# Down projections of an encoder trunk: activations held still and weights moved, with seven products over all inner chunks

## The chip, the cores and the metric

The kernel runs on one core of a Trainium2 chip. The core has a matrix engine (TensorE, PE in the profile), a vector engine (VectorE, DVE), an activation engine (ScalarE, ACT), a general engine (GpSimd, POOL) and a queue engine for transfers (SyncE, SP). Matmuls write into PSUM banks; everything else works in SBUF. The metric is the device time of one execution in microseconds, the median of several runs.

## The reference

The program is a two-layer bidirectional encoder on 512 tokens of width 1024 in float32. Each layer adds, in turn, half of a SwiGLU feed-forward block, an attention mixer, half of a second feed-forward block, and a gated embedding of the layer's own input. Four feed-forward blocks are run in all:

```python
def swiglu(x, w_gate, w_up, w_down):
    return (jax.nn.silu(x @ w_gate) * (x @ w_up)) @ w_down

h = h + 0.5 * swiglu(rmsnorm(h, norm_ffn1[i]), ffn1_w_gate[i], ffn1_w_up[i], ffn1_w_down[i])
```

The inner width is 2816, which is 22 chunks of 128. The down projection is the last product, 512 x 2816 by 2816 x 1024.

## The kernel before

The hidden state is kept feature by token: chunk c of `h` is a tile of 128 features by 512 tokens. Every float32 operand of a matmul is split into a high and a low part (`split`, lines 149 to 151: ScalarE copies the rounded high part, VectorE subtracts it), and every product is made of three matmuls: high by high, high by low and low by high. All weights are split on the chip as they arrive. A raw weight tile (`wr`, five buffers) holds 128 x 1024 numbers, its parts `wh` and `wl` have four buffers each. Activation tiles of 128 x 512 come from a pool `act` of 62 buffers, scratch tiles from `tmp` with eight.

`ffn` first makes the 22 inner chunks, `pair_fast` (line 331) for most of them: gate and up products by a scheme of seven half-size products in place of eight, with sums of weights made partly by an accumulating DMA on GpSimd's queue (line 341). Each chunk is split into `a[m] = (high, low)`, and the first eight are also written to DRAM.

`down` (line 421) then makes the eight output chunks of 128 features by 512 tokens. Weights are the stationary operand and activations move. Output chunks 0 and 1 are plain: 22 inner chunks, three matmuls of 512 columns each (`plain`, lines 440 to 442). Output chunks 2 to 7 go in pairs: the first eight inner chunks by seven products of 256 columns (`product`, lines 484 to 486, with sums of weights from `inner_weights` and of activations from `inner_sums`), the other fourteen plainly. As an output chunk ends, `evict` (line 448) adds half of it to `h`, stores it, and gives the norm's input split (`norm_split`, lines 201 and 202) and its square sum (`norm_square`, line 216, mostly on GpSimd) to the next stage. The next stage (attention projections after the first block of a layer, the gated embedding after the second) starts with `project` or `mm_unit` on these split chunks (`mm3`, lines 175 to 177).

Nothing here writes out the queues by hand, except for a few marked places. A planner orders the instructions of each engine ahead of time, in the program's order of priority and by its own estimate of when inputs and buffers are ready. On the chip each engine then runs its queue strictly in that order, and an instruction whose semaphore is not there yet holds what is behind it.

## Time and profile before

| | |
|---|---|
| median of three runs | 2040.51 us (2040.38 to 2041.76) |
| span of the profiled execution, first to last instruction | 2039.8 us |
| TensorE busy | 2018.5 us, 99% |
| VectorE busy | 1510.8 us, 74% |
| ScalarE busy | 1056.6 us, 52% |
| GpSimd busy | 269.2 us, 13% |
| mean DMA rate | 153 GB/s |

The profile names a group of instructions by its line in the kernel, its engine, its operation and its tiles (output, arrow, inputs). The profiled execution carries no second clock: its own time is the span in the table, 0.7 us under the median of the runs. Matmuls are pipelined, so their durations overlap each other, and the step from one start to the next tells their price.

### The profile page before, as it was taken

How to read it: one execution, taken by the hardware profiler on the slowest of the kernel's cores; microseconds unless marked ns; L12 is line 12 of the kernel's file. 1: busy time of each engine (PE TensorE's matmuls, PEld its weight loads, DVE VectorE, ACT ScalarE, POOL GpSimd, SP SyncE). 2: the span in 40 equal slices, each digit the busy share in tenths (PEclk: the TensorE clock that was granted, in tenths of full speed). 3: DMA queues.
4: the chain of work that ended last, by engine and by line, in shares of the span. 5: the costliest groups of instructions: out<-in, count | busy, mean ns of one | idle time of the engine just before them, and what ended most of it. 6: DMA issues, size and time to landing. Idle time of an engine off the chain costs nothing.

```text
span 2039.8 us, 33724 instructions
## 1 busy us (share of the span) xinstructions
PE 2018.5 (99%) x12862; PEld 1820.6 (89%) x12862; DVE 1510.8 (74%) x2575; ACT 1056.6 (52%) x1798; POOL 269.2 (13%) x306
## 2 busy tenths in 40 slices
PE   9999999999999999999999999999999999999998
PEld 6999988878888899988888999888888889998886
DVE  8888865598766888875568888755778688888554
ACT  6555543377644555553445555434666545555342
POOL 1100011342212110001211100021000111000111
PEclk9999999999999999999999999999999999999999
DMA  7776644543424477653545765545333446665451
GB/s 222 192 187 184 186 142 159 143 98 73 100 72 165 134 197 183 170 191 123 184 152 154 197 182 158 191 143 154 110 104 110 155 127 188 184 180 164 132 204 42
DMA packets 122354, 312.93 MB, mean 153 GB/s; under 512 B 23504, under 2 KB 31184, under 8 KB 122192
## 3 DMA queue, kind: packets, MB, share of 16 engines
q1 hardware_dynamic: 102336, 249.91, 37.6%
q0 software_dynamic: 19712, 60.83, 15.4%
q8 instruction: 101, 1.65, 0.3%
q14 instruction: 61, 0.50, 0.1%
q10 hardware_dynamic: 144, 0.04, 0.0%
HBM read 274.02 MB, written 25.66 MB: 147 GB/s over the span
## 4 chain that ended last, share of the span: by engine, by line
PE 90%; DVE 3%; DMA 2%; ACT 2%; issue 1%; POOL 1%; SPq 0%; DVEq 0%; POOLq 0%; ACTq 0%
PE mm L365 6%; PE mm L364 6%; PE mm L363 6%; PE mm L176 6%; PE mm L177 6%; PE mm L175 6%; PE mm L440 5%; PE mm L441 5%; PE mm L442 5%; PE sc L364 3%; PE sc L363 3%; PE sc L365 3%; PE sc L175 3%; PE sc L177 3%; PE sc L176 3%; PE ob L365 2%
## 5 line engine op out<-in xcount | busy, mean ns | idle before, releaser
L150 ACT ACTIVATE wh<-wr 128x1024 fp32r<-128x1024 f32 (+2 forms) x455 | 465.6, 1026 | 533.6 <-PE mm L441 162.6
L151 DVE TENSOR_TENSOR wl<-wr,wh 128x1024 fp32r<-128x1024 f32 (+2 forms) x455 | 538.3, 1187 | 193.5 <-ACT wh L150 189.9
L365 PE MATMUL mm<-act,wl 128*128 128x256 f32 x1088 | 307.9, 283 | 0.0
L364 PE MATMUL mm<-act,wh 128*128 128x256 f32 x1088 | 307.9, 283 | 0.0
L363 PE MATMUL mm<-act,wh 128*128 128x256 f32 x1088 | 307.9, 283 | 0.0
L175 PE MATMUL mm<-act,wh 128*128 128x512 f32 (+1 forms) x648 | 254.0, 393 | 1.0 <-ACT wh L150 0.5
L176 PE MATMUL mm<-act,wh 128*128 128x512 f32 (+1 forms) x648 | 254.1, 392 | 0.6 <-DVE act L202 0.6
L177 PE MATMUL mm<-act,wl 128*128 128x512 f32 (+1 forms) x648 | 253.7, 392 | 0.0
L364 PEld LDWEIGHTS mm<-act,wh 128*128 128x128 f32 x1088 | 208.8, 192 | 0.3
L363 PEld LDWEIGHTS mm<-act,wh 128*128 128x128 f32 x1088 | 208.9, 192 | 0.2
L365 PEld LDWEIGHTS mm<-act,wl 128*128 128x128 f32 x1088 | 208.9, 192 | 0.2
L440 PE MATMUL mm<-act,wh 128*128 128x512 f32 x512 | 199.4, 389 | 0.0
L441 PE MATMUL mm<-act,wh 128*128 128x512 f32 x512 | 199.4, 389 | 0.0
L442 PE MATMUL mm<-act,wl 128*128 128x512 f32 x512 | 199.2, 389 | 0.0
L150 ACT ACTIVATE act<-tmp 128x512 fp32r<-128x512 f32 (+1 forms) x204 | 113.9, 590 | 85.5 <-DVE tmp L524 36.8
L363 PE MATMUL sc<-act,wh 128*128 128x256 f32 x544 | 154.0, 283 | 0.0
L364 PE MATMUL sc<-act,wh 128*128 128x256 f32 x544 | 154.0, 283 | 0.0
L365 PE MATMUL sc<-act,wl 128*128 128x256 f32 x544 | 154.0, 283 | 0.0
L176 PEld LDWEIGHTS mm<-act,wh 128*128 128x128 f32 x648 | 122.2, 189 | 24.7 <-DVE act L202 2.0
L175 PEld LDWEIGHTS mm<-act,wh 128*128 128x128 f32 x648 | 122.2, 189 | 23.8 <-ACT wh L150 1.0
L177 PEld LDWEIGHTS mm<-act,wl 128*128 128x128 f32 x648 | 122.2, 189 | 22.0 <-DVE wl L151 0.2
L151 DVE TENSOR_TENSOR act<-tmp,act 128x512 fp32r<-128x512 f32 (+1 forms) x200 | 125.4, 641 | 10.4 <-ACT act L150 8.8
(225 smaller groups left out, 4431.7 us busy)
## 6 DMA issues: line engine op xcount, KB each, us to landing
wr<-in_gu_dram SPq DMA_DIRECT2D x176, 512.0 KB, 4.6
wr<-in_gu_dram POOLq DMA_DIRECT2D x68, 512.0 KB, 5.5
wr<-in_dn_dram SPq DMA_DIRECT2D x64, 512.0 KB, 3.9
rb<-in_gu_dram SPq DMA_DIRECT2D x68, 256.0 KB, 2.9
wr<-in_dn_dram SPq DMA_DIRECT2D x32, 384.0 KB, 3.3
wr<-in_qk_ab_dram SPq DMA_DIRECT2D x20, 512.0 KB, 3.5
inner<-tmp POOLq DMA_DIRECT2D x32, 256.0 KB, 3.1
tmp<-inner SPq DMA_DIRECT2D x32, 256.0 KB, 4.4
```

Of the source, the lines that this page charges most:

```text
L150: self.put(self.nc.scalar.activation(hi, src, AF.Copy))
L151: self.put((lo_eng or self.nc.vector).tensor_tensor(lo, src, hi.bitcast(F32), op=ALU.subtract))
L175: mm(out, stat[0], mov[0], start=start, stop=False)
L176: mm(out, stat[0], mov[1], start=False, stop=False)
L177: return mm(out, stat[1], mov[0], start=False, stop=stop)
L363: mm(out, w[0][:, c], xs[k][0][:, x], start=start and k == 0, stop=False, skip_group_check=True)
L364: mm(out, w[0][:, c], xs[k][1][:, x], start=False, stop=False, skip_group_check=True)
L365: mm(out, w[1][:, c], xs[k][0][:, x], start=False, stop=stop and k == half - 1, skip_group_check=True)
L440: mm(p, u[0][:, c], xh, start=start and j == 0, stop=False, skip_group_check=True)
L441: mm(p, u[0][:, c], xl, start=False, stop=False, skip_group_check=True)
L442: mm(p, u[1][:, c], xh, start=False, stop=s + j == NF - 1, skip_group_check=True)
```

## The change

The down projection is turned around. A tile of activations (128 inner by 128 tokens) is now the stationary operand, and the weights move, 512 output columns at a time, so that an output block is 128 tokens by 512 features. Tokens, inner width and output width are each cut in two, and the whole product is made of seven products of quarter blocks (256 tokens, 11 inner chunks, 512 features) in four sections. The first section makes two products per weight quarter, the second one, the third three, the fourth one. Sums of weight quarters are made in the raw tile by accumulating DMAs on GpSimd's queue (`add`), sums of activations by GpSimd's own operations in place (`pool`), and VectorE and ScalarE split every result. `ffn` no longer splits the inner chunks, nor writes them to DRAM. The weights are laid out on the host as four quarters.

The output quarters are put together on ScalarE and VectorE, turned back to feature by token with 32 transposes on TensorE (`turned`), and added to `h` (`done`), for the last four chunks in token halves, so `norm_split` takes a range of tokens. `mm_units` is new: the stages that follow make their first two projections together, chunks 0 to 3 for both, then chunks 4 to 7.

```diff
...
 FRONT = 4
 FAST = range(5, NF)
 SUMS = 0, 1, 2, 3
-SEVEN = 4
-LATER = 3, 4, 5
-READY = 3
+K2 = NF // 2
 UP_AT = 3
 LEAD = 6
 ACTS = 62
...
         mm(out, stat[0], mov[1], start=False, stop=False)
         return mm(out, stat[1], mov[0], start=False, stop=stop)
-    def mm_unit(self, out, u, xs, start, stop):
-        for i, x in enumerate(xs):
+    def mm_unit(self, out, u, xs, start, stop, ks=None):
+        for i in ks or range(len(xs)):
             w = (u[0][:, i * P:(i + 1) * P], u[1][:, i * P:(i + 1) * P])
-            self.last_mm = self.mm3(out, w, x, start and i == 0, stop and i == len(xs) - 1)
+            self.last_mm = self.mm3(out, w, xs[i], start and i == 0, stop and i == len(xs) - 1)
+    def mm_units(self, outs, us, between=None):
+        half = KC // 2
+        for ks in (range(half), range(half, KC)):
+            for out, u in zip(outs, us):
+                self.mm_unit(out, u, self.xg, True, True, ks)
+            if between:
+                between()
+                between = None
     def begin_norm(self, k):
...
         self.norm_split(c)
         self.norm_square(c)
-    def norm_split(self, c):
-        nc = self.nc
-        h, g = self.h[c], self.gain[:, self.k, c:c + 1]
+    def norm_split(self, c, x=slice(0, T)):
+        nc = self.nc
+        h, g = self.h[c][:, x], self.gain[:, self.k, c:c + 1]
         if self.k < N_NORM - 1:
-            hi, lo = self.act(F32R), self.act(F32R)
-            ins = (self.put(nc.scalar.activation(hi, h, AF.Copy, scale=g)),
-                   self.put(nc.vector.scalar_tensor_tensor(lo, h, g, hi.bitcast(F32), op0=ALU.mult, op1=ALU.subtract)))
-            self.xg[c] = (hi, lo)
-            return ins
+            if self.xg[c] is None:
+                self.xg[c] = self.act(F32R), self.act(F32R)
+            hi, lo = (y[:, x] for y in self.xg[c])
+            return (self.put(nc.scalar.activation(hi, h, AF.Copy, scale=g)),
+                    self.put(nc.vector.scalar_tensor_tensor(lo, h, g, hi.bitcast(F32), op0=ALU.mult, op1=ALU.subtract)))
     def norm_square(self, c):
         nc = self.nc
...
         a, y, t = [], [None] * KC, [None] * (KC // 2)
         kept = io["xT"].rearrange("p c t -> c p t") if first else self.put_away()
-        raw = self.dp.tile([2 * SEVEN, P, T], F32, name=self.nm("inner"))
         for m in range(NF):
             if m < FRONT:
                 r = self.pair_front(gu[i, m], m, first, gu[i, m + 1])
...
                 r = self.pair_fast(gu[i, m], y, t)
             else:
                 r = self.pair(gu[i, m], y)
-            if m < 2 * SEVEN:
-                nc.gpsimd.dma_start(raw[m], r)
-            ah, al = self.act(F32R), self.act(F32R)
-            self.split(r, ah, al)
-            a.append((ah, al))
+            a.append(r)
             for c, after in enumerate(SUMS):
                 if m == after:
                     y[c], y[c + KC // 2], t[c] = self.halves(c)
         self.begin_norm(k_next)
-        self.down(dn[i], a, raw, kept)
-    def down(self, w, a, raw, kept):
+        self.down(dn[i], a, kept)
+    def down(self, w, a, kept):
         nc, H = self.nc, T // 2
         l, r = slice(0, H), slice(H, T)
         self.kept = self.dp.tile([KC, P, T], F32, name=self.nm("kept"))
...
+        copy, tt, sub = nc.scalar.activation, nc.vector.tensor_tensor, ALU.subtract
+        pool = nc.gpsimd.tensor_tensor
+        b11, b12, b21, b22 = (w[n] for n in range(4))
+        units = [slice(u, min(u + 2, K2)) for u in range(0, K2, 2)]
+        ks = lambda u: range(u.start, u.stop)
+        def load(b, u):
+            raw = self.wr.tile([P, UNIT], F32, tag="wr", name=self.nm("wr"))[:, :(u.stop - u.start) * T]
+            nc.sync.dma_start(raw, b[:, u.start * T:u.stop * T])
+            return raw
+        def add(raw, b, u):
+            nc.gpsimd.dma_start(raw, b[:, u.start * T:u.stop * T], accum_op=ALU.add)
+        def product(out, u, ws, xs, cols, start, stop):
+            mm = nc.tensor.matmul
+            for j, k in enumerate(ks(u)):
+                wh, wl = (x[:, j * T:(j + 1) * T] for x in ws)
+                for i, p in enumerate(out):
+                    c = slice(cols.start + i * P, cols.start + (i + 1) * P)
+                    xh, xl = (x[:, c] for x in xs[k])
+                    mm(p, xh, wh, start=start and k == 0, stop=False, skip_group_check=True)
+                    mm(p, xh, wl, start=False, stop=False, skip_group_check=True)
+                    mm(p, xl, wh, start=False, stop=stop and k == K2 - 1, skip_group_check=True)
+        def copied(p):
+            out = [self.act() for _ in p]
+            for o, x in zip(out, p):
+                copy(o, x, AF.Copy)
+            return out
+        r1, r3 = [self.bank(), self.bank()], [self.sbank(), self.sbank()]
+        x1, x2, x3, x4 = ([None] * K2 for _ in range(4))
+        for u in units:
+            raw = load(b11, u)
+            for k in ks(u):
+                pool(a[k][:, r], a[k][:, r], a[K2 + k][:, r], op=sub)
+                x1[k] = self.split_chunk(a[k], nc.vector)
+            product(r1, u, self.parts(raw), x1, l, True, True)
+            add(raw, b12, u)
+            product(r3, u, self.parts(raw), x1, r, True, True)
+        c1, c5 = copied(r1), copied(r3)
+        r2 = [self.bank(), self.obank()]
+        for u in units:
+            raw = load(b21, u)
+            for k in ks(u):
+                x2[k] = self.split_chunk(a[K2 + k], nc.vector)
+            product(r2, u, self.parts(raw), x2, l, True, True)
+        for o, p in zip(c1, r2):
+            tt(o, p, o, op=ALU.add)
+        c11 = c1
+        rb, rc = [self.tbank(), self.tbank()], [self.bank(), self.obank()]
+        for u in units:
+            raw = load(b12, u)
+            add(raw, b22, u)
+            for k in ks(u):
+                pool(a[k][:, r], a[k][:, r], a[k][:, l], op=sub)
+                pool(a[k][:, l], a[k][:, r], a[K2 + k][:, r], op=ALU.add)
+                x3[k] = self.split_chunk(a[k], nc.vector)
+                pool(a[K2 + k][:, l], a[K2 + k][:, l], a[k][:, r], op=ALU.add)
+            product(rb, u, self.parts(raw), x3, l, True, True)
+            add(raw, b11, u)
+            product(r1, u, self.parts(raw), x3, r, False, True)
+            add(raw, b21, u)
+            product(rc, u, self.parts(raw), x2, r, True, True)
+        c2, c21 = copied(r1), [self.act(), self.act()]
+        u3 = [self.act(), self.act()]
+        for i in range(2):
+            tt(u3[i], c2[i], rb[i], op=sub)
+            tt(c21[i], rc[i], u3[i], op=ALU.add)
+            tt(c5[i], c5[i], u3[i], op=sub)
+        c22 = c5
+        hs = []
+        for m in range(KC):
+            hs.append(self.act())
+            nc.sync.dma_start(hs[m], kept[m])
+        for u in units:
+            raw = load(b22, u)
+            for k in ks(u):
+                hi, lo = self.act(F32R), self.act(F32R)
+                self.split(a[K2 + k][:, l], hi[:, l], lo[:, l])
+                x4[k] = hi, lo
+            product(r3, u, self.parts(raw), x4, l, False, True)
+        def turned(out, x, j):
+            for i, y in enumerate(x):
+                nc.tensor.transpose(out[:, i * P:(i + 1) * P], y[:, j * P:(j + 1) * P], self.ident)
+        def done(m, p, c):
+            h = hs[m]
+            nc.vector.scalar_tensor_tensor(h[:, c], p, 0.5, h[:, c], op0=ALU.mult, op1=ALU.add)
             self.h[m] = h
-            if m not in LATER:
+            if c.stop == T and c.start == 0:
                 self.norm_split(m)
+            else:
+                self.norm_split(m, c)
+        M = KC // 2
+        for m in range(M):
+            p = self.tbank()
+            turned(p[:, l], c11, m)
+            turned(p[:, r], c21, m)
+            done(m, p, slice(0, T))
+            nc.gpsimd.dma_start(self.kept[m], hs[m])
             self.norm_square(m)
...
+        for m in range(0, M, 2):
+            p = self.tbank()
+            for j in range(2):
+                turned(p[:, j * H:(j + 1) * H], c22, m + j)
+            for j in range(2):
+                done(M + m + j, p[:, j * H:(j + 1) * H], r)
+        for c in (l, r):
+            for i in range(2):
+                tt(c2[i][:, c], r3[i][:, c], c2[i][:, c], op=sub)
+        for m in range(0, M, 2):
+            p = self.tbank()
+            for j in range(2):
+                turned(p[:, j * H:(j + 1) * H], c2, m + j)
+            for j in range(2):
+                done(M + m + j, p[:, j * H:(j + 1) * H], l)
+        for m in range(M, KC):
+            nc.gpsimd.dma_start(self.kept[m], hs[m])
+            self.norm_square(m)
     def parts(self, raw):
         n = raw.shape[-1]
...
-        p = [self.project(w[12 + i], self.sbank()) for i in range(2)]
+        p = [self.obank(), self.bank()]
+        self.mm_units(p, [self.unit(w[12 + i], lo_eng=self.lo_eng()) for i in range(2)])
...
+        first = [self.obank(), self.bank()]
+        self.mm_units(first, [self.unit(io["qk_c"][i], lo_eng=self.lo_eng()) for i in range(2)])
         fill, steps = [], []
         for n in range(KC):
-            fill += [(("q", n), 1, lambda n=n: proj_q(n)), (("k", n), 1, lambda n=n: proj_k(n))]
+            fill += [(("q", n), 1, lambda n=n: proj_q(n, None if n else first[0])),
+                     (("k", n), 1, lambda n=n: proj_k(n, None if n else first[1]))]
...
-        up, ends = None, []
+        up, ends, first = None, [], []
         for m in range(KC):
             self.fetch(self.kept, m)
-            u = self.unit(io["plg"][i, m])
+            u = first[m][0] if m < len(first) else self.unit(io["plg"][i, m])
             if m % 4 == 0:
                 up = self.unit(io["plp"][i, m // 4])
             s = m % 4 * 2 * P
             upm = tuple(x[:, s:s + 2 * P] for x in up)
+            if m == 0:
+                first = [(u, self.bank(), self.obank()), (self.unit(io["plg"][i, 1]), self.bank(), self.sbank())]
+                def inner():
+                    for j, (_, _, q) in enumerate(first):
+                        self.mm_unit(q, tuple(x[:, j * 2 * P:(j + 1) * 2 * P] for x in up), p, True, True)
+                self.mm_units([f[1] for f in first], [f[0] for f in first], inner)
             half = k_next == N_NORM - 1 and m == KC - 1
             for x in (slice(0, T // 2), slice(T // 2, T)) if half else (slice(0, T),):
                 cut = lambda parts: [tuple(y[:, x] for y in c) for c in parts]
-                pg, pp = self.bank()[:, x], self.sbank()[:, x]
-                self.mm_unit(pg, u, cut(xg), True, True)
-                self.mm_unit(pp, upm, cut(p), True, True)
+                if m < len(first):
+                    pg, pp = first[m][1:]
+                else:
+                    pg, pp = self.bank()[:, x], self.sbank()[:, x]
+                    self.mm_unit(pg, u, cut(xg), True, True)
+                    self.mm_unit(pp, upm, cut(p), True, True)
                 if m == 0:
                     R = self.R
                     self.begin_norm(k_next)
...
     return np.concatenate([u[:, :, D // 2:], u[:, :, :D // 2], g], axis=2)
+def _quarters(w):
+    return w.reshape(2, K2, P, 2, T).transpose(0, 3, 2, 1, 4).reshape(4, P, K2 * T)
 def _rows(w):
     k, m = w.shape
...
     for n, (wg, wu, wd) in (("1", (ffn1_w_gate, ffn1_w_up, ffn1_w_down)),
                             ("2", (ffn2_w_gate, ffn2_w_up, ffn2_w_down))):
         a["gu" + n] = np.stack([_pairs(wg[i], wu[i]) for i in range(DEPTH)])
-        a["dn" + n] = np.stack([_tiles(wd[i]) for i in range(DEPTH)])
+        a["dn" + n] = np.stack([_quarters(wd[i]) for i in range(DEPTH)])
```

More of the change, by code (lines that the diff above doesn't have):

```diff
@@ L282, in pair_front @@
         R = self.R
-        t1, t2 = self.tmp(), self.tmp()
+        t1, t2 = self.tmp(), self.act()
         nc.vector.tensor_tensor(t1, pgu[0], R, op=ALU.mult)
@@ L304, in pair @@
             pgu.append(p)
-        t = self.tmp()
+        t = self.act()
         nc.scalar.activation(t, pgu[0], AF.Silu)
```

109 lines of the change are left out of this document (5 added, 104 removed).

## Prediction

> **What bounds the kernel now.** I read the shares of the engines first, then the groups of the down projection, then the order of time around one of its four calls.
>
> ```profile
> span 2039.8 us, 33724 instructions
> PE 2018.5 (99%) x12862; PEld 1820.6 (89%) x12862; DVE 1510.8 (74%) x2575; ACT 1056.6 (52%) x1798; POOL 269.2 (13%) x306
> L440 PE MATMUL mm<-act,wh 128*128 128x512 f32 x512 | 199.4, 389 | 0.0
> L484 PE MATMUL mm<-act,wh 128*128 128x256 f32 x144 | 40.8, 283 | 0.0
> L484 PE MATMUL sc<-act,wh 128*128 128x256 f32 x144 | 40.7, 283 | 0.0
> L484 PE MATMUL ob<-act,wh 128*128 128x256 f32 x48 | 13.6, 283 | 0.0
> ```
>
> TensorE is never free, and the last column says that no matmul of the down projection waited. Three lines (440 to 442) issue 512 matmuls each of 512 columns, three (484 to 486) issue 336 each of 256 columns: 384 and 252 in each call. Their mean durations (389 and 283 ns) overlap, so a matmul's price is the step from one start to the next:
>
> ```profile
> 237.97 0.28 PE L364 MATMUL mm<-act,wh 128*128 128x256 f32 x1
> 238.09 0.28 PE L365 MATMUL mm<-act,wl 128*128 128x256 f32 x1
> 238.22 0.40 PE L440 MATMUL mm<-act,wh 128*128 128x512 f32 x1
> 238.45 0.40 PE L441 MATMUL mm<-act,wh 128*128 128x512 f32 x1
> ...
> 354.45 0.39 PE L441 MATMUL mm<-act,wh 128*128 128x512 f32 x1
> 355.36 0.39 PE L442 MATMUL mm<-act,wl 128*128 128x512 f32 x1
> 355.58 0.39 PE L175 MATMUL sc<-act,wh 128*128 128x512 f32 x1
> ```
>
> 256 columns step by 0.12 us, 512 by 0.2275 (354.45 to 355.36 is four steps). The call runs from 238.22 to 355.58, 117.4 us; 384 x 0.2275 + 252 x 0.12 = 117.6. So the call is matmul steps and nothing else, and a split of weights or activations, a DMA or a sum costs nothing as long as it stays beneath them. The change is worth what it takes from the steps, less what it brings out from beneath.
>
> **The change, part by part.**
>
> *Matmuls.* All 22 chunks go through seven products of 11 chunks, two blocks of 128 tokens and three terms: 7 x 11 x 2 x 3 = 462 matmuls of 512 columns in a call. 462 x 0.2275 = 105.1 us. Added are 32 transposes of 128 by 128 in a call. The trace has such transposes in the attention:
>
> ```profile
> 415.00 0.60 PE L663 MATMUL tr<-ident,act 128*128 128x128 f32 x4
> ```
>
> Four take 0.60 us where one alone takes 0.275, so the step is (0.60 - 0.275)/3 = 0.108 us, and 32 cost 3.5 us. 105.1 + 3.5 = 108.6, against 117.4: **8.8 us less per call, 35 us in four**. This is the gain if nothing new shows.
>
> *What FFN loses.* The split of each of the 22 inner chunks, the eight writes and eight reads of inner chunks and their subtractions leave the gate and up products or the old down call. They lie beside matmuls with no idle, so they are worth nothing in time. The change moves 11 splits of 2 halves into the new call and multiplies the weight splits, which is the cost to look at.
>
> *VectorE and GpSimd.* The prices:
>
> ```profile
> 272.27 2.29 DVE L151 TENSOR_TENSOR wl<-wr,wh 128x1024 fp32r<-128x1024 f32 x2 [0.82 <-ACT wh L150]
> 287.98 0.69 DVE L449 SCALAR_TENSOR_TENSOR tmp<-mm,tmp 128x512 f32<-128x512 f32 x1 [1.99 <-PE mm L442]
> 288.59 0.68 DVE L151 TENSOR_TENSOR wl<-wr,wh 128x512 fp32r<-128x512 f32 x1
> ...
> 290.58 1.78 DVE L539 TENSOR_TENSOR wr<-wr,wr 128x512 f32<-128x512 f32 x1
> 290.11 1.70 POOL L216 TENSOR_TENSOR ssq<-ssq,tmp 128x512 f32<-128x512 f32 x1 [0.58 <-ACT tmp L209]
> 632.15 1.28 POOL L216 TENSOR_TENSOR ssq<-ssq,tmp 128x512 f32<-128x512 f32 x1 [45.25 <-ACT tmp L209]
> 632.18 1.80 DVE L202 SCALAR_TENSOR_TENSOR act<-act,gain,act 128x512 fp32r<-128x512 f32 x1
> 100.00:210.00 110.00, 110.00 (x919) 110.00 (x918) 91.87 (x129) 62.51 (x97) 10.07 (x12) 1.00 0.71 187
> ```
>
> A weight split of 1024 columns steps by 1.145 us (two in 2.29), an operation of 512 columns by 0.61 (287.98 to 288.59), one of 256 I take at 0.34, between half of that and the whole. L539 and L202 start while a GpSimd sum runs and end 0.55 us after it has ended: two operations that read and write SBUF on these two engines exclude each other. GpSimd's sum alone takes 1.28 us for 512 columns; the change's 44 GpSimd sums a call have 256, whose cost lies between 0.64 and 1.28. I take 0.64, half of the nearest row for half the columns; at 1.28 the third section below would want 21 us more, which I leave out of the range. So the sums must be added to VectorE's time. By section (first: two products per weight quarter; second: one; third: three; fourth: one):
>
> First: TensorE 132 x 0.2275 = 30.0 us; 11 weight splits 12.6 + 11 chunk splits 6.7 + 11 GpSimd sums 7.0 = 26.3. Second: TensorE 15.0; 6.3 + 6.7 + two sums from PSUM 1.2 = 14.2. Third: TensorE 45.0; 18.9 + 6.7 + six combinations 3.7 + 33 GpSimd sums 21.1 = 50.4. Fourth: TensorE 15.0; 6.3 + 3.7 = 10. The first three together want 90.9 of the 90.0 us that TensorE needs. The third alone is 5.4 over. Some of it can run early: nine or ten of the first section's sums have their inputs before the gate and up products end, where VectorE is busy 91.9 of 110 us and TensorE loses nothing (the window's row has, after its length, the busy us of PE, PEld, DVE, ACT and POOL, then clock, DMA share and GB/s). That takes about 6 us off and leaves 85 of 90. No part of the old kernel ran the two engines at 94% with TensorE behind them. Bounds: nothing when the order of the queues is ideal, 5.4 a call when the third section gets no help. I take 2 us.
>
> *ScalarE* has one pass for each of VectorE's splits, and nothing shared; at 62.5 of 110 us in the same window it stays behind VectorE, and I cost it at nothing.
>
> *DMA.* Weight sums come from accumulating DMAs on GpSimd's queue. A call moves each quarter (2.88 MB) twice: four plain loads, four accumulates, against 11.5 MB plain before.
>
> ```profile
> DMA packets 122354, 312.93 MB, mean 153 GB/s; under 512 B 23504, under 2 KB 31184, under 8 KB 122192
> q1 hardware_dynamic: 102336, 249.91, 37.6%
> q0 software_dynamic: 19712, 60.83, 15.4%
> wr<-in_gu_dram SPq DMA_DIRECT2D x176, 512.0 KB, 4.6
> wr<-in_gu_dram POOLq DMA_DIRECT2D x68, 512.0 KB, 5.5
> L341 POOL DMA_DIRECT2D wr<-in_gu_dram x68: 841/866/952, 31.6 to 1819.0; - x68
> ```
>
> The plain queue takes 37.6% of 2039.8 us for 249.91 MB, 3.07 us a MB on all 16 engines; GpSimd's, mostly accumulates, 15.4% for 60.83 MB, 5.16 us a MB. First section: 2.88 x 8.23 = 23.7 of 30.0 us. Second: 8.9 of 15.0. Third, one load and three accumulates: 8.9 + 44.6 = 53.5 of 45.0. The third is 8.5 us over. Five raw buffers let it start early: a buffer's load and its first accumulate are 0.524 x 8.23 = 4.3 us, and the first two sections leave 12.4 us of DMA time free, so two buffers filled ahead cover it. Bounds: 0 and 8.5 us a call; I take 1, because a unit of two chunks has 8.2 us of matmuls and its chain (4.6 + 3 x 5.5 us of landings, three splits between them) fits 5 buffers x 8.2 = 41 us with room.
>
> The new waits are on GpSimd's in-order queue: an accumulate waits for the split that reads its buffer, and behind it stand GpSimd's sums, and behind these VectorE's chunk splits and the matmuls. A unit of the third section asks 6 x 0.64 + 3 x 0.87 = 6.5 of 8.2 us of that queue.
>
> The Trainium skill (page "SBUF — State Buffer", section "SBUF: two separate sides") warns that GpSimd can't write the descriptors of its DMAs while VectorE holds the shared port, which would put a VectorE operation's wait on each of the 24 accumulates of a call. The trace does not bear it out for these operations: 841 to 952 ns for all 68, beside a VectorE that is busy 84% of the time. By the page's rule the third section's GpSimd queue would be 6.5 + 3 x 1.15 = 9.9 us for 8.2 and cost 9 us a call (2061 in all, with the rest of the sum; a chance of 0.02); by the row it costs nothing.
>
> *The turning at the end.* Before, the first matmul of the next stage follows the last of the call by 0.22 us. Now half the output can only be formed after the last product: VectorE has four subtractions (1.4 us), four evictions of 512 columns with their norm splits, and eight of 256 with theirs: 4 x (0.61 + 0.66) + 8 x (0.34 + 0.37) = 10.8, in all 12.2 us, plus about 1.5 us of latency. TensorE has 3.5 us of transposes, 24 matmuls on chunks 0 to 3 for two output blocks (the new helper that takes two units half by half, 5.5 us) and chunk 4 to 6's 18 (4.1): 13.1, and 2.7 more in the per-layer embedding stage. What waits behind is the whole next stage. Bounds 0 to 5; I take 2 us a call, 8 in all. The DMA of this section (2.88 MB and 2.1 MB of h, 15.3 us for 15.0) fits only because h can come early.
>
> **Sum**: against the span of 2039.8, 4 x (-8.8 + 2 + 1 + 2) = -15 gives 2024.6; the median of the runs shown is 0.7 above this span, so **2025 us**.
>
> **The rivals.**
>
> *The floor.* Splits, sums and accumulates all stay beneath, and only about 0.5 us of the end shows: 4 x (-8.8 + 0.5) = -33, 2007 us. For it speaks that the old call hid everything; against it that the call before asked much less of VectorE and half the DMA bytes.
>
> *The third section is DMA-bound.* Its accumulates aren't started ahead, because the raw buffers stay with the second section's loads or because GpSimd's queue stands at an accumulate whose load is late. It decides when fewer than two of the five buffers hold the third section's weights as it begins. Price 8.5 a call, with 2 at the end and 2 of the port: 4 x (-8.8 + 12.5) = +15, **2055 us**; with the port's part beneath the DMA's, 2047. For it: 53.5 us in 45. Against it: the engines aren't full in the first two sections.
>
> *The port is lost to early sums.* GpSimd's sums for the third section are ready as soon as the first has split, and may run in the second, where VectorE is at 14.2 of 15.0. One 0.64 us sum after each operation of 0.61 to 1.145 leaves VectorE about 58%, so the second section would take 14.2/0.58 = 24.5 us, of which four buffers of split weights (4 x 2.7 us) cover part: some 4 to 9 us a call in place of my 2, 2033 to 2053. The same page's section calls the pair of ports an exclusive lock that is held for a whole instruction; the 1.78 us of L539 agrees.
>
> **How the numbers follow.** My forecast (2012 to 2036) has 0.50, the floor 0.14, the DMA-bound section 0.18, the starved descriptors 0.02, the lost port 0.16, whose lower half is no change or a small gain. A measurement of this kernel tells 0.2% (4 us) from no change, so 2036.4 to 2044.6 is "same". Faster: 0.50 + 0.14 and a little of the last, 0.65; same 0.09; slower 0.26. The range runs from the floor's 2005 to 2052, which leaves out the worst of the DMA case. The likeliest one's own range is 2012 to 2036.
>
> **What will show it.** 1848 matmuls of 512 columns on the new product's line at 0.2275 us and 128 transposes at about 0.11 confirm the gain. Idle before matmuls of that line: in the second section, ended by VectorE, it is the port; in the third, ended by a weight split that itself waited for a landing, the DMA; after the last product, ended by the norm splits, the turning. GpSimd sums of 256 columns far over 0.64 us, or weight splits over 1.3, show the exclusion. I am wrong if the matmul step with tokens stationary is not 0.2275, or if more than 8.8 us of idle stands in a call.

## The result, and the profile after

| | before | after |
|---|---|---|
| median | 2040.45 us (2039.88 to 2041.76) | 2455.86 us (2453.61 to 2457.63) |
| after over before, 95% interval | | 1.2036 (1.2019 to 1.2053) |
| span of the profiled execution | 2039.8 us | 2455.9 us |
| TensorE busy | 99% | 88% |

The change costs 415 us, 104 us in each of the four calls. The forecast was 2025 us with a range up to 2052, so it was wrong by sign and far outside its range. The head of the page of the kernel after and its two large DMA queues:

```profile
span 2455.9 us, 32981 instructions
PE 2155.1 (88%) x12294; PEld 1839.0 (75%) x12294; DVE 1627.9 (66%) x2571; ACT 1130.8 (46%) x1902; POOL 487.0 (20%) x534
...
q1 hardware_dynamic: 97728, 241.52, 30.6%
q0 software_dynamic: 30016, 95.44, 22.7%
```

No engine is full, and the two queues together take 53% of the DMA engines' time, as they did before (37.6% + 15.4%). A kernel that got slower with no engine full waits on a chain. The stage that waits is found by windows over the four sections of the first call (length; busy us and count of TensorE, weight loads, VectorE, ScalarE and GpSimd; granted clock; DMA share; GB/s):

```profile
238.00:298.00 60.00, 41.43 (x135) 29.68 (x133) 26.70 (x24) 16.71 (x23) 23.15 (x25) 0.83 0.45 90
298.00:319.00 21.00, 17.53 (x68) 12.11 (x69) 18.86 (x19) 13.65 (x22) 11.99 (x13) 1.00 0.85 224
319.00:434.00 115.00, 73.35 (x216) 50.77 (x215) 40.20 (x43) 26.36 (x33) 16.20 (x21) 0.75 0.52 108
434.00:451.00 17.00, 17.00 (x69) 13.92 (x68) 14.54 (x22) 11.18 (x21) 4.04 (x5) 0.88 0.70 253
```

TensorE needs 30, 15, 45 and 15 us for these sections. The first takes twice that and the third two and a half times, and these are the two sections with accumulating DMAs. Sections two and four, which only load, are near what they need (the second also takes the third's first accumulates). In the third, TensorE (73 us, partly at a lower clock), VectorE (40), ScalarE (26), GpSimd (16) and DMA (0.52) are all idle for a good part of 115 us. The granted clock is low in both long sections (0.83 and 0.75), but TensorE stands idle for 18.6 us of the one and 41.7 us of the other, so the lower clock does not set their length. Who waits for whom is in the view of waits (engine and tile, what it waited for, us in all, times, longest):

```profile
DVE wl L149 <- ACT wh L148: 503.9, 215, 8.7
ACT wh L148 <- DMA wr<-in_dn_dram: 472.2, 76, 9.1
POOL wr L443 <- DVE wl L149: 449.3, 60, 9.4
```

These three close a ring: the split waits for a landing in the raw tile, the accumulate on GpSimd waits for the split, and the next landing is that accumulate. The time line of the first section shows one turn of it (start, length, engine, line; in brackets the idle time before and what ended it):

```profile
267.26 2.01 ACT L148 ACTIVATE wh<-wr 128x1024 fp32r<-128x1024 f32 x2 [7.99 <-DMA wr<-in_dn_dram]
268.35 2.36 DVE L149 TENSOR_TENSOR wl<-wr,wh 128x1024 fp32r<-128x1024 f32 x2 [7.52 <-ACT wh L148]
...
271.01 0.87 POOL L443 DMA_DIRECT2D wr<-in_dn_dram  x1 [8.99 <-DVE wl L149]
276.71 2.00 ACT L148 ACTIVATE wh<-wr 128x1024 fp32r<-128x1024 f32 x2 [7.44 <-DMA wr<-in_dn_dram]
277.80 2.36 DVE L149 TENSOR_TENSOR wl<-wr,wh 128x1024 fp32r<-128x1024 f32 x2 [7.08 <-ACT wh L148]
```

ScalarE's two splits (x2) stand back to back: the summed tile of unit u, for which it waited 7.99 us, and right behind it the plain tile of unit u+1, whose load was long there. VectorE does the same two, GpSimd issues the accumulate into u+1 only as they end (270.7), and 5.7 us after its start at 271.01 ScalarE splits the tile that it fills: the ring turns again. One turn is 276.71 - 267.26 = 9.45 us, for a unit with 24 x 0.2275 = 5.46 us of matmuls. In program order the summed tile of u stands ahead of the plain tile of u+1, and the queues kept that order. So five raw tiles were there, and one chain was under way at a time.

In the third section the first accumulates of five units had gone out ahead (between 305 and 321 us), and the ring makes two turns a unit for the other two:

```profile
352.23 2.00 ACT L148 ACTIVATE wh<-wr 128x1024 fp32r<-128x1024 f32 x2 [7.25 <-DMA wr<-in_dn_dram]
361.87 1.06 ACT L148 ACTIVATE wh<-wr 128x1024 fp32r<-128x1024 f32 x1 [7.64 <-DMA wr<-in_dn_dram]
370.03 2.00 ACT L148 ACTIVATE wh<-wr 128x1024 fp32r<-128x1024 f32 x2 [7.11 <-DMA wr<-in_dn_dram]
```

From pair to pair it is 17.80 us, for a unit with 36 x 0.2275 = 8.19 us of matmuls.

What was foreseen of the matmuls holds. The time line of TensorE at the end of the fourth section:

```profile
450.34 0.39 PE L452 MATMUL sc<-wh,act 128*128 128x512 f32 x1
450.57 0.39 PE L453 MATMUL sc<-wl,act 128*128 128x512 f32 x1
450.80 0.39 PE L454 MATMUL sc<-wh,act 128*128 128x512 f32 x1
451.03 0.71 PE L520 MATMUL tr<-ident,act 128*128 128x128 f32 x5
```

The step is 0.23 us, and a transpose (0.71 - 0.275)/4 = 0.109. The groups of the new work (line, engine, shapes, count; busy us, mean ns; idle before and its releasers):

```profile
L452 PE MATMUL mm<-wh,act 128*128 128x512 f32 x264 | 127.1, 506 | 141.2 <-ACT wh L148 136.2 <-ACT act L148 4.9
L452 PE MATMUL sc<-wh,act 128*128 128x512 f32 x176 | 78.4, 469 | 73.2 <-ACT wh L148 73.2
...
L443 POOL DMA_DIRECT2D wr<-in_dn_dram x96 | 85.2, 888 | 477.5 <-DVE wl L149 449.3 <-DVE act L149 19.2 <-DMA wr<-in_dn_dram 7.4
L492 POOL TENSOR_TENSOR act<-act,act 128x256 f32<-128x256 f32 x44 | 50.2, 1212 | 45.5 <-DVE act L149 45.5
L489 POOL TENSOR_TENSOR act<-act 128x256 f32<-128x256 f32 x44 | 48.7, 1140 | 9.6 <-DVE act L149 9.6
L490 POOL TENSOR_TENSOR act<-act,act 128x256 f32<-128x256 f32 x44 | 43.9, 1034 | 1.6
L467 POOL TENSOR_TENSOR act<-act,act 128x256 f32<-128x256 f32 x44 | 32.2, 733 | 257.9 <-DVE act L398 257.9
```

The mean of a matmul is 506 and 469 ns where it was 389: part of them run at a lower clock (0.83 and 0.75 in the windows of the first and third section). A GpSimd sum of 256 columns takes 0.73 us in the first section's group, most of which runs while the gate and up products still go on, and 1.03 to 1.21 us in the third's, beside VectorE.

### The profile page after: what moved, and what is told of

The parts are those of the page before. It is cut to its first block, busy times and chain, and to the rows that moved or that the text cites. A ratio compares the mean times of both kernels' runs of the same rounds, so it can differ in the third digit from the quotient of the medians.

```text
span 2455.9 us, 32981 instructions
## 1 busy us (share of the span) xinstructions
PE 2155.1 (88%) x12294; PEld 1839.0 (75%) x12294; DVE 1627.9 (66%) x2571; ACT 1130.8 (46%) x1902; POOL 487.0 (20%) x534
## 3 DMA queue, kind: packets, MB, share of 16 engines
q0 software_dynamic: 30016, 95.44, 22.7%
## 5 line engine op out<-in xcount | busy, mean ns | idle before, releaser
L149 DVE TENSOR_TENSOR wl<-wr,wh 128x1024 fp32r<-128x1024 f32 (+1 forms) x503 | 611.2, 1222 | 504.9 <-ACT wh L148 503.9
L148 ACT ACTIVATE wh<-wr 128x1024 fp32r<-128x1024 f32 (+1 forms) x503 | 511.6, 1028 | 833.6 <-DMA wr<-in_dn_dram 472.2
L452 PE MATMUL mm<-wh,act 128*128 128x512 f32 x264 | 127.1, 506 | 141.2 <-ACT wh L148 136.2
L452 PEld LDWEIGHTS mm<-wh,act 128*128 128x128 f32 x264 | 58.4, 233 | 181.9 <-ACT wh L148 163.6
L149 DVE TENSOR_TENSOR act<-act,act 128x512 fp32r<-128x512 f32 (+1 forms) x192 | 180.5, 985 | 13.5 <-ACT act L148 13.4
L443 POOL DMA_DIRECT2D wr<-in_dn_dram x96 | 85.2, 888 | 477.5 <-DVE wl L149 449.3
L349 POOL DMA_DIRECT2D wr<-in_gu_dram x68 | 60.0, 882 | 494.6 <-DMA wr<-in_gu_dram 251.8
```

The costliest lines, as they stand in the source:

```text
L148: self.put(self.nc.scalar.activation(hi, src, AF.Copy))
L149: self.put((lo_eng or self.nc.vector).tensor_tensor(lo, src, hi.bitcast(F32), op=ALU.subtract))
L349: nc.gpsimd.dma_start(rs, w[:, :UNIT], accum_op=ALU.add)
L443: nc.gpsimd.dma_start(raw, b[:, u.start * T:u.stop * T], accum_op=ALU.add)
L452: mm(p, xh, wh, start=start and k == 0, stop=False, skip_group_check=True)
```

## The experiments

The theory after the first look was that the program's order makes the chains run one after another. The rivals: the bytes of the accumulates at their low rate; GpSimd's sums and the port that they share with VectorE; GpSimd's in-order queue; the turning. Times below are differences of ratios, each to the runs of the kernel before on the same chip, times 2040.5 us; the interval of each ratio is about 6 us to either side. Lengths of sections are taken from the starts of a call's matmuls 1, 133, 199, 397 and its last, in the first call unless said. "Tail" is the time from that last matmul to the 48th 512-column matmul of the next stage: 10.9 us for these and 3.5 for transposes make 14.4. It is the same where the embedding follows: there twelve of the 48 are products with the embedding's own input.

| kernel | median, us | ratio (95%) | sections, us |
|---|---|---|---|
| after | 2455.86 | 1.2036 (1.2019 to 1.2053) | 60.2, 20.4, 115.4, 16.6 |
| no accumulates | 2088.43 | 1.0238 (1.0208 to 1.0268) | 33.9, 17.5, 54.9, 16.4 |
| order apart by one | 2146.86 | 1.0525 (1.0494 to 1.0555) | 36.5, 19.3, 64.1, 16.7 |
| order apart by two | 2159.40 | 1.0586 (1.0555 to 1.0617) | 36.6, 18.9, 67.5, 16.5 |
| sums on VectorE | 2431.07 | 1.1918 (1.1883 to 1.1952) | 55.0, 22.7, 113.6, 15.9 |
| apart, early splits | 2136.71 | 1.0454 (1.0424 to 1.0485) | 36.7, 18.8, 56.2, 14.7 |
| same, no accumulates | 2074.92 | 1.0152 (1.0123 to 1.0181) | 33.3, 17.5, 45.1, 14.7 |
| same, no sums | 2100.68 | 1.0278 (1.0248 to 1.0308) | 31.4, 15.6, 57.6, 14.7 |
| same, neither | 2062.80 | 1.0093 (1.0063 to 1.0122) | 31.4, 15.7, 44.9, 14.7 |
| early splits, norm sums on VectorE | 2126.53 | 1.0411 (1.0380 to 1.0441) | 36.4, 20.4, 55.4, 14.7 |
| early splits, half accumulates | 2113.40 | 1.0346 (1.0316 to 1.0376) | 37.4, 19.1, 49.2, 14.7 |
| early splits, six raw tiles | 2131.77 | 1.0436 (1.0406 to 1.0467) | 36.5, 19.0, 54.9, 14.7 |

**No accumulates.** The order of the change stays, and the landings are taken away.

```diff
 def add(raw, b, u):
-    nc.gpsimd.dma_start(raw, b[:, u.start * T:u.stop * T], accum_op=ALU.add)
+    pass
```

> The changed kernel without any of the accumulating DMAs of the down projection: each raw weight tile is split again and again as it was loaded, so the products use unsummed weights (the sums are left out, the output is another). Everything else stays. Serial chain of accumulates (my theory): the first section falls from 60 us to about 30, the third from 115 to about 45 to 50, so some 100 us a call and a time of about 2040 to 2060. DMA rate: the same fall, since the bytes go too. GpSimd against VectorE: the sums of activations stay, so the third section would stay near 100 us and the time over 2350.

367 us of the 415 go. The accumulates, or what waits for them, are nearly all of the loss; 49 us over the kernel before stay, more than the 0 to 20 expected, and the third section keeps 54.9 us where 45 to 50 were expected. This run alone can't tell their bytes from their place in the order.

**Order apart.** The bytes and the work stay; only the program's order changes. In the first section the second product of a unit is issued two units later; in the third the three products of a unit stand one unit apart, and loads with their first accumulate are issued two units ahead. The edit is shown shortened.

```diff
+SKEW1, SKEW3, LEAD3 = 2, 1, 2
...
     product(r1, u, self.parts(raw), x1, l, True, True)
     add(raw, b12, u)
-    product(r3, u, self.parts(raw), x1, r, True, True)
+pend.append((u, raw))
+if len(pend) > SKEW1:
+    v, old = pend.pop(0)
+    product(r3, v, self.parts(old), x1, r, True, True)
...
+begin(n + LEAD3 - 1)                       # load b12, add b22
 product(rb, units[n], ...); add(raws[n], b11, units[n])
+product(r1, units[n - SKEW3], ...); add(raws[n - SKEW3], b21, ...)
+product(rc, units[n - 2 * SKEW3], ...)
```

> All work, bytes and results of the changed kernel, in another program order: in the first section the product with the summed weights comes two units after the plain one of its unit; in the third section the three products of a unit come one unit apart, and loads and first accumulates two units ahead. Serial chain: accumulates of different units overlap, first section about 32 us, third about 55 to 75 (a round still waits for one accumulate of 6 to 7 us per unit), time about 2100 to 2200. DMA rate: the bytes are the same, so the third section stays near 115 and the time over 2400. GpSimd against VectorE: the same, over 2400.

The windows of its first and third section, to be set against 60.0 and 115.0 us above:

```profile
237.80:274.30 36.50, 32.10 (x134) 25.69 (x133) 30.24 (x25) 18.14 (x27) 26.51 (x26) 0.95 0.70 162
...
293.60:357.80 64.20, 53.39 (x223) 42.09 (x222) 37.18 (x45) 26.16 (x35) 15.75 (x19) 0.89 0.87 196
```

The first section falls by 23.5 us and the third by 51, the kernel by 308 us (77 a call). The third section's transfers move at 196 GB/s in place of 108. ScalarE's wait for landings and GpSimd's for splits fall with it:

```profile
ACT wh L149 <- DMA wr<-in_dn_dram: 164.6, 48, 11.7
POOL wr L444 <- DVE wl L150: 118.6, 35, 9.0
```

They were 472 and 449 us. So the order is shown to be the cause of three quarters of the loss.

**Apart by two**, with the lead cut to one unit (`SKEW1, SKEW3, LEAD3 = 2, 2, 1`):

> As the one before, with the three products of a unit of the third section two units apart, loads and first accumulates one unit ahead. Serial chain: twice the time for each accumulate, but five raw tiles are all in use, so the next load waits for a release: third section 50 to 75 us, time 2080 to 2200. DMA rate and GpSimd against VectorE: over 2400, as before.

12 us slower than apart by one, with intervals that just touch, and the third section 3.4 us longer. More distance within a unit was paid for here with less lead between units; the two were changed together and not told apart.

**Sums on VectorE**, in the order of the change:

```diff
-pool = nc.gpsimd.tensor_tensor
+pool = nc.vector.tensor_tensor
```

> The changed kernel with the 44 sums of activations of a call on VectorE in place of GpSimd. Serial chain: VectorE stands idle in the first and third section, so the time stays within 2% of 2456, and only the second section (20.4 us) may move by a few us. GpSimd against VectorE: 44 blockings of 0.7 us or more go, the third section falls by 20 us or more, time under 2370. DMA rate: no change.

24 us faster than the change, and the third section still takes 113.6 us. Accumulates that stand behind sums on GpSimd's queue, and the port, are at most a small part of the loss in this order.

**Apart, and the fourth section's splits early.** On top of the order apart by one, the splits of the fourth section's chunks stand behind the third's last product of each unit, and `h` is fetched there.

```diff
+for k in ks(u):
+    t = self.act(F32R)
+    self.split(a[K2 + k][:, l], t[:, l], t[:, r])
+    x4[k] = t[:, l], t[:, r]
+if n == 4: (loads of hs)
```

> The order with rounds apart by one, and in it the fourth section's activation splits made as the third section frees its tiles, high and low part in one tile, and the loads of h moved into the third section. If the 10 us between the third and the fourth section are a shortage of activation tiles, they shrink to about 1 and the time falls from 2147 by 25 to 40 us, to 2107 to 2122. If the transposes stand there for another reason, it stays within 10 us of 2147.

Expected were 25 to 40 us, and it gained 14 by the ratios, between the two forecasts. The third section lost 8 us, but most of that is a move: the transposes that had stood between sections three and four went to the end, where the tail of the first call grew from 13.8 to 20.9 us. Sections and tail together went from 150.5 to 147.2. But this order holds all matmuls of the product together, and so is the base on which the suspects are taken out one by one.

**Neither, or one, of accumulates and sums.** The sums are taken out with `pool = lambda *x, **kw: None`, the accumulates as in the first experiment.

> The kernel before this one in the list without its accumulating DMAs (sums of weights left out, another output). What the accumulates still cost when they overlap: if the chain is out of the way, first to third section fall together by under 5 us a call; if the third section is bound by the DMA rate (53.5 us asked of 45), by 8 us a call or more, over 32 us in the time.

> The same order with accumulates, without the 44 sums of activations on GpSimd in each call (sums left out, another output). If GpSimd and VectorE exclude each other, VectorE loses 28 to 32 us of blocking a call, and first and second section fall by 4 to 8 us a call together, 16 to 32 us in the time. If the sums lie beside the matmuls as I put it, less than 2 us a call.

> The same order without accumulates and without sums (both left out, another output). Matmuls, weight splits, activation splits, copies and the turning are left: sections 30, 15, 45 and 15 us if nothing else binds, that is 105 us a call, and a time of 2005 to 2025. If it stays over 2040, a cost that I have not named stands beside the two.

The window of the third section with both accumulates and sums (the kernel with early splits):

```profile
293.70:349.90 56.20, 48.99 (x199) 38.33 (x198) 32.09 (x42) 24.54 (x38) 14.26 (x17) 0.94 0.92 207
```

The same window without accumulates:

```profile
288.60:333.70 45.10, 45.10 (x200) 37.11 (x199) 33.55 (x45) 25.70 (x38) 0.14 (x1) 1.00 0.37 117
```

The same window without sums:

```profile
285.20:342.80 57.60, 49.82 (x200) 39.35 (x199) 31.02 (x43) 25.95 (x39) 12.11 (x14) 0.91 0.92 213
```

And the windows of the first three sections without either:

```profile
239.20:270.60 31.40, 30.12 (x135) 24.61 (x133) 20.28 (x24) 18.69 (x27) 0.00 (x0) 1.00 0.39 117
270.60:286.20 15.60, 15.45 (x66) 12.32 (x67) 14.29 (x20) 12.57 (x20) 0.00 (x0) 1.00 0.44 136
286.20:331.10 44.90, 44.90 (x199) 37.16 (x199) 31.14 (x42) 26.04 (x39) 0.00 (x0) 1.00 0.36 118
```

Without accumulates TensorE is full in the third section (45.10 of 45.10). Without sums it is as long as with them, at the same DMA share of 0.92. So in this order the accumulates hold the third section, and the sums do not; at a share of 0.92 the likely limit is the DMA engines. The accumulates cost 62 us beside the sums (1.0454 to 1.0152), 15 a call, 11 of them in the third section; without the sums beside them they cost 38 us (1.0278 to 1.0093).

The sums cost 12 us without accumulates (1.0152 to 1.0093), 3 a call, and these lie in the first two sections (33.3 and 17.5 against 31.4 and 15.7), none in the third. Beside accumulates they cost 36 us (1.0454 to 1.0278), 9 a call, 8.5 of them in the first two sections (36.7 and 18.8 against 31.4 and 15.6). That is a little more than the 4 to 8 us expected of those two sections. How much of it is VectorE's port and how much GpSimd's queue wasn't told apart.

Without either, all four sections are within 1.4 us of what TensorE needs, and still the kernel is 0.9% slower than before, at 2063 us where 2005 to 2025 were expected if nothing else bound. The rest is at the end of the call and behind it: the tails are 20.9, 25.3, 21.9 and 24.8 us, where 14.4 are needed, a loss of 6.5, 10.9, 7.5 and 10.4 us. The two longer ones, ahead of the embedding, are also those with the lower granted clock: 0.87 and 0.80 in the second and the fourth, 1.00 and 0.97 in the others.

**What holds the tail.** The time line of this kernel as a call ends:

```profile
349.52 0.74 DVE L213 SCALAR_TENSOR_TENSOR act<-act,gain,act 128x512 fp32r<-128x512 f32 x1
...
350.46 1.31 POOL L225 TENSOR_TENSOR ssq<-ssq,tmp 128x512 f32<-128x512 f32 x1
350.78 1.55 DVE L213 SCALAR_TENSOR_TENSOR act<-act,gain,act 128x512 fp32r<-128x512 f32 x1
```

A norm split takes 0.74 us alone and 1.55 where GpSimd adds a square sum: the two of them exclude each other, now on the path, since TensorE waits for these splits. So the square sums of this place were given to VectorE.

```diff
-eng = nc.vector if c == KC - 1 or self.k == 0 else nc.gpsimd
+eng = nc.vector if c == KC - 1 or self.k == 0 or self.k % 2 else nc.gpsimd
```

> The order with rounds apart by one and early splits, with the square sums of the norm that follows a down projection on VectorE in place of GpSimd. If the end of a call is long because GpSimd's seven sums of 1.3 us hold VectorE's norm splits up, VectorE gains 7 x (1.3 - 0.61) = 4.8 us a call there, the 48 matmuls after the last product take 16 to 18 us in place of 21 and 25, and the time falls by 12 to 25 us, to about 2112 to 2125. If the end is VectorE's own work and latency, VectorE has 4.3 us more to do and the end gets longer.

The rows show the splits at 0.75 us and the sums at 0.69:

```profile
369.68 0.69 DVE L225 TENSOR_TENSOR ssq<-ssq,tmp 128x512 f32<-128x512 f32 x1
370.28 0.75 DVE L213 SCALAR_TENSOR_TENSOR act<-act,gain,act 128x512 fp32r<-128x512 f32 x1
```

The tails went from 20.9, 25.5, 21.5 and 24.9 to 18.5, 24.2, 18.6 and 24.7 us. The median is 10 us lower where 12 to 25 were expected, and the two intervals overlap. In the attention stages little of the loss is left: the first tail now also holds 27 matmuls of 256 columns of the work behind (3.2 us at 0.12), and TensorE is busy for 18.35 of the 18.70 us from 365.3 on. In the embedding stages the tail hardly moved, so the square sums are not what holds it; the granted clock is 0.90 and 0.87 there, and what starts the gaps was not settled.

**Half the accumulated bytes, and a sixth raw tile.** If the third section is bound by bytes, half of them should bring it down and another buffer should not.

```diff
-nc.gpsimd.dma_start(raw, b[:, u.start * T:u.stop * T], accum_op=ALU.add)
+n = (u.stop - u.start) * T // 2
+nc.gpsimd.dma_start(raw[:, :n], b[:, u.start * T:u.start * T + n], accum_op=ALU.add)
```

> The same order with every accumulate on half the columns of its tile: as many accumulates and waits, half their bytes (half of the sums of weights left out, another output). If the third section (56 us) is now bound by the DMA rate, it asks 8.9 + 22.3 = 31 us and falls to 45 to 48, the time by 30 to 45 us. If each round still waits for its own accumulate, whose landing of 6 to 8 us falls by 1.5 us at most, the section stays over 51 us.

```diff
-SKEW1, SKEW3, LEAD3 = 2, 1, 2
+SKEW1, SKEW3, LEAD3 = 2, 1, 3
-ACTS = 62
+ACTS = 60
-WR = 5
+WR = 6
```

> The same order with six raw weight tiles in place of five (and two activation tiles fewer), loads and first accumulates three units ahead, all bytes. DMA rate: the bytes are the same, so the third section stays within 2 us of 54 to 56 (or loses what one tile more loaded ahead, 4.3 us, can save). Waiting for single accumulates: one unit more in flight cuts it to under 49 us.

The third section goes from 56.2 to 49.2 us with half the bytes, and to 54.9 with the sixth tile (the kernel with six tiles can't be told from the one with five). Its window with half the bytes:

```profile
294.40:343.60 49.20, 46.66 (x200) 36.86 (x199) 33.09 (x44) 25.73 (x39) 11.93 (x14) 1.00 0.75 169
```

That lies between what was expected of the rate (45 to 48) and of waits for single accumulates (over 51), and the time fell by 22 us by the ratios where 30 to 45 were expected. So bytes are most of the 11 us that the accumulates cost there. At a DMA share of 0.75 the remaining 4 us over TensorE's 45 are hardly the rate any more; what they are was not tried.

**The ledger.** Against a kernel that gains the whole 8.8 us a call (2005 us), a call of the change loses 113 us, which the differences of the runs share out: 81 to the order (after against early splits; 77 of them by apart by one), 15 to the accumulates, 3 to the sums, and 13.5 to what stays without either. With the sums taken out first, accumulates and sums are 9 each. Of the last, about 9 are the tails, 1.6 the sections, and some 3 lie in the stages behind the tails. From a call's last product to the next call's first, or to the end, the kernel without either takes 14.6, 17.5, 11.8 and 17.3 us more than the kernel before; without the transposes and the tails' loss that leaves 4.6, 3.1, 0.8 and 3.4. It goes with the clock: after the first, second and fourth tail the trace has 3.4 us at half the clock (from 383.4, 1021.7 and 2004.8 us), after the third none. What the gaps ahead of them wait for was not settled. No version beat the kernel before: the one without accumulates and sums is already 0.9% slower.

## Why the prediction was wrong

*The matmuls.* Right: 616 matmuls on each of three lines in all, 0.2275 us a step, transposes at 0.109. Where nothing else binds, the sections take 31.4, 15.7, 44.9 and 14.7 us for 30, 15, 45 and 15. The gain is there; in the fastest version that does all the work, the one with the norm's sums on VectorE (84 us over before, 21 a call), the rest costs 30 us a call against these 8.8.

*The DMA term, "a unit of two chunks has 8.2 us of matmuls and its chain (4.6 + 3 x 5.5 us of landings, three splits between them) fits 5 buffers x 8.2 = 41 us with room".* **This is the step that failed.** The price of a link was right to the size: a landing and two splits make the ring's turn of 9.45 us. But to divide by five buffers takes five chains under way, and the number under way is set by the order in which the in-order queues hold the splits, not by the number of raw tiles. The diff shows that order: `product` on the plain tile, `add`, `product` on the summed tile, next unit. The prediction quoted a wait of this kind as a danger to GpSimd's queue, and priced what that queue has to do (6.5 of 8.2 us) rather than what each of its accumulates waits for. Its bounds of 0 to 8.5 us a call came from bytes; the runs show 77 to 81 for the order.

*The rival that the third section is DMA-bound.* Its price was 8.5 us a call (53.5 us asked of 45), and once the order is mended it is what one finds: 53.5 to 57.0 us in the four calls, at 0.92 of the DMA engines in the first. The rate of 5.16 us a MB, read from the trace before, was near enough for this section: 0.92 of 56.2 us is 51.7 us of the DMA engines. It is a mean over a queue that also carried plain transfers, and in the kernel after, with more accumulates on it, that queue took 5.84 us a MB (22.7% of 2455.9 us for 95.44 MB). The reason against it, that two tiles filled ahead cover it, did not. As the main case it would have given 2055 us, still 400 off, for the order hides it. (The range's lower end, called the floor's 2005, is the whole gain of 8.8 us a call; the floor itself was priced at 2007.)

*VectorE and GpSimd.* I took 2 us a call, with 5.4 as the bound; without accumulates it is 3, beside them 9, in the first two sections and not in the third, which I had called 5.4 over. The price of a sum was mis-sized: 0.64 taken, 0.73 measured in the first group and 1.03 to 1.21 in the third's, 44 us a call in place of 28. The rival of early sums, 4 to 9 us with the second section at 24.5, did not come in that form: the section took 20.4 us in the kernel after and 17.5 without accumulates. Its size was nearer than mine, for with early splits the sums cost 8.5 us in the first two sections together, 3.2 of them in the second.

*Starved descriptors.* Not seen. The median of 96 accumulate issues is 866 ns, as it was before:

```profile
L443 POOL DMA_DIRECT2D wr<-in_dn_dram x96: 866/866/1202, 235.8 to 2344.2; - x96
```

The page of the Trainium skill named in the prediction ("SBUF — State Buffer") says further down, under "Who interferes with whom", that a VectorE operation with two SBUF inputs contends with GpSimd's reads; that descriptors are left alone by it is given there as an inference. The row agrees with that: 32 of the 96 issues lie for more than half of their length beside a VectorE operation with two inputs, with a median of 881 ns, against 866 for the others. I had taken the warning too widely.

*The turning.* I took 2 of 0 to 5 us; the tails lose 6.5 to 10.9 with all sums and accumulates gone, over the upper bound. Missing from the sum of 12.2 us were the norm splits at 1.55 us beside GpSimd's square sums, though the prediction had quoted that exclusion for another place. They were nearly all of the loss in the attention stages; in the embedding stages they were not, and what was stays open.

*What was to show it.* "More than 8.8 us of idle in a call" and "idle before matmuls, ended by a weight split that itself waited for a landing" are what the groups and the waits show, 136 us and 73 us of idle in the four calls on line 452 alone.

## What to carry to other kernels

A buffer count is not a pipeline depth: before dividing a chain by its buffers, write down the order in which each in-order engine meets the steps of two neighbouring units, and look whether the last step of one stands ahead of the first step of the next. A sum made in place by a DMA is a round trip through issue, landing and split, so its second use belongs units later in the program. And price the end of a stage by itself when work that formed output all along is gathered there: its cost shows even when every matmul section is full.

## What the runs showed of the hardware

A gap of under 2 us can cost TensorE more than its own length. The time line of the kernel after, around a wait for the norm's column:

```profile
1216.86 0.40 PE L173 MATMUL mm<-act,wh 128*128 128x512 f32 x1
1219.02 0.65 PE L250 MATMUL tr<-ident,rcol 128*128 128x128 f32 x4 [1.77 <-POOL rcol L234]
1219.42 0.60 PE L174 MATMUL mm<-act,wh 128*128 128x512 f32 x1
1219.82 0.63 PE L175 MATMUL mm<-act,wl 128*128 128x512 f32 x1
1220.25 0.63 PE L173 MATMUL mm<-act,wh 128*128 128x512 f32 x1
...
1222.81 0.50 PE L173 MATMUL mm<-act,wh 128*128 128x512 f32 x1
1223.15 0.39 PE L174 MATMUL mm<-act,wh 128*128 128x512 f32 x1
1223.38 0.39 PE L175 MATMUL mm<-act,wl 128*128 128x512 f32 x1
```

After 1.77 us of idle the 512-column step is 0.427 us ((1222.81 - 1220.25)/6) in place of 0.23, and is back 3.7 us after the first of them (1219.42 to 1223.15). Eight such steps cost 1.6 us beyond the gap. The window from 1219 to 1223 has it as a granted clock of 0.58, which is half the clock for 3.4 of its 4 us:

```profile
1219.00:1223.00 4.00, 3.98 (x13) 3.20 (x14) 0.69 (x1) 2.48 (x3) 0.00 (x0) 0.58 0.39 131
```

The Trainium skill (page "TensorE: Matmul & The Clock Gate", section "What's actually happening") has TensorE fall to half its clock after an idle window of about 3.4 us, and come back after as long a stretch of work. The way back agrees with 3.7 us here; the gap ahead of it was 1.77 us, about half of what the page names. Not every such gap does it: of the 22 idle stretches of 1.5 to 2 us that begin at full clock in the kernel after, 11 are followed by a fall within 3.5 us of their end, and of the 17 of 2 to 2.5 us, 15.

The other surprise is the rate of accumulating DMAs under load: in a good order the third section moved 207 GB/s at a share of 0.92, where the fourth section of the kernel after, without accumulates of weights, moved 253 at 0.70. So here GB/s did not tell how full the DMA engines were, where a part of the transfers accumulates; the share did.
